# Third step of the common product placed behind P4 of both groups, in the last pair of each SwiGLU

## The chip, the cores and the metric

One core of one Trainium2 chip runs the whole program. The metric is the device time of the program in microseconds, as a median of several runs. Engines are named as the profile names them: PE multiplies matrices, DVE and ACT work on vectors, SP issues the transfers (DMAs).

## The reference

The program is one layer of an encoder block on a sequence of 1024 tokens with 1024 channels, in float32: a SwiGLU, a token-mixing layer (retention and pooling), and a second SwiGLU.

```
h = x + 0.5 * swiglu(rmsnorm(x), ffn1_w_in, ffn1_w_out)
...
h = h + mixing(rmsnorm(h))
h = h + 0.5 * swiglu(rmsnorm(h), ffn2_w_in, ffn2_w_out)
out = rmsnorm(h)

def swiglu(x, w_in, w_out):            # w_in: 1024 x 5632, w_out: 2816 x 1024
    gate, up = split(x @ w_in, 2)
    return (silu(gate) * up) @ w_out
```

The change concerns `x @ w_in`, the first product of each SwiGLU. What it computes is not changed.

## The kernel before

**Three matmuls for one.** Each float32 operand is split into a rounded part and a rest (`split`, lines 160 to 162: a cast on ACT, then a subtraction on DVE). A product of two such operands is three matmuls (`mm3`, lines 181 to 183).

**Groups.** The first product of a SwiGLU makes 22 groups of hidden channels, one by one or in pairs. A group takes two 128-channel tiles (its gate and its up) and all tokens and channels, and is computed by a scheme of Strassen's kind (`strassen`): seven products instead of eight, numbered 1 to 7 and written P1 to P7, each of twelve 512-wide matmuls. Step `A[6]` of a group `A` is P4; it adds into the group's bank `e` and evacuates it, as the (1, 0) quarter, into `au` (line 761). Names in the first SwiGLU begin with `a`, in the second with `c`; the second products (`ffn_out`) are `b` and `d`.

**Pairs and their common product.** Two groups A and B have one more product, P3, in common (`common`): a further split into 2 x 2 smaller blocks saves one of eight. It has three steps, each with a preparation (of weights, on ACT and DVE) and a body (on PE, with the evacuation):

- `one` writes two banks, `x` and `y`, and adds into A's bank `b`.
- `two` finishes A's bank `b`. It also adds `y2` into the lower half of bank `x`, which DVE then reads (line 619, `tt(t["A"][:, HI], x[:, LO], ...)`); then A's `finish` adds bank `b` onto the gate (line 761).
- `three` adds `y4` into B's bank `b` and `y3` into the same half of bank `x`. ACT copies that half (line 627), DVE adds it (line 628), and B's `finish` adds B's bank `b` (line 761).

When both a group's P4 and its `finish` have run, `end` puts its remaining work in a list: the scaling with the norm (line 775), the Silu (line 783), the multiplication with `up` (line 781), and sums and stores for the second product.

**Order.** `pairs_of_both` yields steps in the order in which PE shall do them. `Flow.run` issues the preparation of a step four steps (`LOOK`) before its body, and after each body some of the listed work. A scheduler then sets the order on each engine from these, with the work inside `soon()` (evacuations) ahead of the rest. In all pairs that share P3, `parted` puts A's P4 between `two` and `three`; B's P4 follows.

**Banks.** PE writes into eight banks: six of the pool `ps` and two of the pool `sum` (`N_PS, N_SUM = 6, 2`). A's and B's `b` are the two `sum` banks. The second product begins with four banks `a` (P1) and four banks `b` (P6), which stay in use for all of its eleven steps; the first two `b` banks are the `sum` banks again:

```
bk[where, i] = (sum_bank if where == "b" and i < N_SUM else bank)(f"{name}{n}{where}{i}")
```

A step of the second product is P1 (`bp1a`) and P6 (`bp6b`), twelve matmuls each, three for each bank. Their operands are split by ACT and DVE too (`bp1w`, `bp1m`, `bp6w`, `bp6m` with the number of the step), and lines 906 to 908 make sums of weights.

## Time and profile before

| | |
|---|---|
| median of 3 runs | 2072.68 us (2071.74 to 2073.24) |
| the profiled execution, its own time | 2071.6 us |
| its span in the trace | 2069.8 us |
| granted clock of PE, mean | 0.999 |
| moved by DMAs | 313.57 MB, mean 151 GB/s |

The page of the profile gives busy times by engine, a chain of waits, and groups of instructions. The trace behind it can be asked for the instructions of an engine in order of time (the timeline), for who waited for whom (the waits), and for busy times and the granted clock in stretches (the windows). In a timeline row stand the start and the duration in us, the engine, the line, the operation, its output and inputs (without buffer numbers), and in brackets idle time before it and what ended it. The first SwiGLU's last pair ends at about 407 us of the span, the second's at about 1857 us.

### The profile page before, as it was taken

What the parts mean: (1) busy time and instruction counts of PE and PEld (TensorE: products, weight loads), DVE (VectorE), ACT (ScalarE), POOL (GpSimd) and SP (SyncE); (2) the same over time, 40 slices, a digit from 0 to 9 for tenths busy, and PEclk for the clock granted to TensorE, in tenths of its full rate; (3) what the DMA queues carried; (4) which work ended last, traced back from release to release, by engine and by line L of the source; (5) the groups of instructions that cost most, each with busy time, mean ns of one, the idle gap of its engine ahead of it and who ended that gap; (6) DMA issues with size and microseconds to landing.
All of it is one profiled execution on the core that took longest, in us unless ns stands there. A gap on an engine that the chain in (4) does not pass through costs nothing.

```text
span 2069.8 us, 29688 instructions
## 1 busy us (share of the span) xinstructions
PE 2044.7 (99%) x10672; PEld 1811.1 (87%) x10672; DVE 1835.8 (89%) x3262; ACT 1091.3 (53%) x2061; POOL 0.2 (0%) x4
## 2 busy tenths in 40 slices
PE   9999999999999999999999999999999999999998
PEld 7888989888888888888888999888789999988887
DVE  8799898998996798999778888999989989899897
ACT  8545444554654535454447763456645545455454
POOL 0000000000000000000000000000000000000000
PEclk9999999999999999999999999999999999999999
DMA  7232424576542323243337566724224232457642
GB/s 263 82 138 77 143 87 142 200 265 203 179 151 94 120 106 130 91 143 120 119 128 236 188 234 235 253 92 162 72 86 137 91 136 87 134 207 267 216 145 100
DMA packets 118819, 313.57 MB, mean 151 GB/s; under 512 B 13200, under 2 KB 17424, under 8 KB 118672
## 3 DMA queue, kind: packets, MB, share of 16 engines
q1 hardware_dynamic: 118096, 310.64, 44.4%
q8 instruction: 83, 1.36, 0.3%
q10 hardware_dynamic: 576, 1.05, 0.1%
q14 instruction: 64, 0.52, 0.1%
HBM read 220.93 MB, written 90.70 MB: 151 GB/s over the span
## 4 chain that ended last, share of the span: by engine, by line
PE 74%; DVE 18%; issue 3%; DMA 3%; ACT 3%; SPq 0%; ACTq 0%; DVEq 0%
PE c_b L181 2%; PE c_b L182 2%; PE c_b L183 2%; PE a_b L181 2%; PE a_b L182 2%; PE a_b L183 2%; PE c_e L183 1%; PE c_e L182 1%; PE c_e L181 1%; PE a_e L181 1%; PE a_e L182 1%; PE a_e L183 1%; PE dp5a L181 1%; PE dp5a L182 1%; PE dp5a L183 1%
## 5 line engine op out<-in xcount | busy, mean ns | idle before, releaser
L182 PE MATMUL c_b<-n3T,c_wS 128*128 128x512 f32 x176 | 66.8, 380 | 0.0
L181 PE MATMUL c_b<-n3T,c_wS 128*128 128x512 f32 x176 | 66.5, 380 | 0.2 <-ACT n3T L161 0.2
L183 PE MATMUL c_b<-n3T,c_wS 128*128 128x512 f32 x176 | 66.7, 379 | 0.0
L181 PE MATMUL a_b<-n1T,a_wS 128*128 128x512 f32 x168 | 63.7, 379 | 0.0
L182 PE MATMUL a_b<-n1T,a_wS 128*128 128x512 f32 x168 | 63.7, 379 | 0.0
L183 PE MATMUL a_b<-n1T,a_wS 128*128 128x512 f32 x168 | 63.7, 379 | 0.0
L181 PE MATMUL a_a<-n1R,a_wL 128*128 128x512 f32 x120 | 45.5, 379 | 0.0
L182 PE MATMUL a_a<-n1R,a_wL 128*128 128x512 f32 x120 | 45.5, 379 | 0.0
L183 PE MATMUL a_a<-n1R,a_wL 128*128 128x512 f32 x120 | 45.5, 379 | 0.0
L182 PE MATMUL c_a<-n3R,c_wL 128*128 128x512 f32 x112 | 42.7, 381 | 1.1 <-DVE n3R L166 1.1
L181 PE MATMUL c_a<-n3R,c_wL 128*128 128x512 f32 x112 | 42.6, 380 | 0.8 <-ACT c_b L521 0.8
L183 PE MATMUL c_a<-n3R,c_wL 128*128 128x512 f32 x112 | 42.5, 379 | 0.0
L181 PEld LDWEIGHTS c_b<-n3T,c_wS 128*128 128x128 f32 x176 | 33.2, 189 | 5.1 <-ACT n3T L161 0.6
L182 PEld LDWEIGHTS c_b<-n3T,c_wS 128*128 128x128 f32 x176 | 33.3, 189 | 4.8 <-DVE n3T L162 0.3
L183 PEld LDWEIGHTS c_b<-n3T,c_wS 128*128 128x128 f32 x176 | 33.3, 189 | 4.6
L162 DVE TENSOR_TENSOR a_wS<-a_S,a_wS 128x512 fp32r<-128x512 f32 x45 | 31.3, 697 | 5.0 <-ACT a_wS L161 4.9
L183 PEld LDWEIGHTS a_b<-n1T,a_wS 128*128 128x128 f32 x168 | 31.8, 189 | 4.5
L182 PEld LDWEIGHTS a_b<-n1T,a_wS 128*128 128x128 f32 x168 | 31.8, 189 | 4.3
L181 PEld LDWEIGHTS a_b<-n1T,a_wS 128*128 128x128 f32 x168 | 31.8, 189 | 4.4
L162 DVE TENSOR_TENSOR c_wS<-c_S,c_wS 128x512 fp32r<-128x512 f32 x46 | 32.0, 698 | 2.4 <-ACT c_wS L161 2.3
L161 ACT CAST c_wS<-c_S 128x512 fp32r<-128x512 f32 x46 | 27.8, 622 | 11.4 <-DVE c_S L484 7.0
L182 PE MATMUL c_e<-n3T,c_wL 128*128 128x512 f32 x88 | 33.5, 380 | 0.1
(3159 smaller groups left out, 8034.8 us busy)
## 6 DMA issues: line engine op xcount, KB each, us to landing
c_ra<-in_f_in SPq DMA_DIRECT2D x22, 512.0 KB, 3.7
c_rb<-in_f_in SPq DMA_DIRECT2D x22, 512.0 KB, 3.8
a_ra<-in_f_in SPq DMA_DIRECT2D x21, 512.0 KB, 3.9
a_rb<-in_f_in SPq DMA_DIRECT2D x21, 512.0 KB, 3.8
t<-au SPq DMA_DIRECT2D x11, 512.0 KB, 2.8
b<-ag SPq DMA_DIRECT2D x11, 512.0 KB, 3.7
r<-au SPq DMA_DIRECT2D x11, 512.0 KB, 3.5
bra<-in_f_out SPq DMA_DIRECT2D x11, 512.0 KB, 5.8
```

Of the source, the lines that this page charges most:

```text
L161: copy(hi, src)
L162: tt(lo, src, hi.bitcast(F32), SUB)
L181: mm(dst, w[0], m[0], start=start, stop=False, skip_group_check=True)
L182: mm(dst, w[0], m[1], start=False, stop=False, skip_group_check=True)
L183: mm(dst, w[1], m[0], start=False, stop=stop, skip_group_check=True)
```

## The change

In the last pair of each first product, and only there, the third step of the common product is yielded after the P4 of both groups:

```diff
             yield from (A[1], B[3], B[1], A[2], B[2])
-            if k != some:
+            if n == len(groups) - 2:
+                steps = common(nx, A, B, 3)
+                yield from (*steps[:2], A[6], B[6], steps[2])
+            elif k != some:
                 yield from parted(common(nx, A, B, 3), A[6])
                 yield B[6]
             else:
```

From line 686 on, lines of the changed kernel have numbers higher by 3: line 761 is 764, 775 is 778, 781 is 784, 783 is 786, 908 is 911. Both kernels have the same number of instructions on every engine. Where the orders differ, in each SwiGLU, is from the last P4 to the first steps of the second product. Rows below are those of the first SwiGLU (A is group 10, B is group 21); those of the second read the same with `c` and `d` for `a` and `b`.

On PE, at the end of the first product, before (the last matmul of A's P4, then the first one of each further product; in brackets the engines whose semaphores it waits for):

```order
L183 MATMUL a10_e_3881<-n1T43_754,a10_wL22_3986 128x512
L181 MATMUL a21_b_3822<-n1R22y4_1268,a10_wy3_4003 128x256 [waits DVE_49]
...
L181 MATMUL a10_x3_4023<-n1R22y3_1260,a10_ws343_3967 128x256 [waits DVE_49]
...
L181 MATMUL a21_e_3947<-n1T40_708,a21_wL22_4020 128x512 [waits Activation_49]
...
L181 MATMUL bp1a0_4163<-bp1m0_4055,bp1w0_4052 128x512 [waits Activation_49]
...
L181 MATMUL bp6b1_4194<-bp6m0_4081,bp6w0_4078 128x512 [waits DVE_49,PE_49]
```

and now:

```order
L183 MATMUL a10_e_3881<-n1T43_754,a10_wL22_3986 128x512
L181 MATMUL a21_e_3947<-n1T40_708,a21_wL22_4003 128x512
...
L181 MATMUL a21_b_3822<-n1R22y4_1268,a10_wy3_4020 128x256 [waits Activation_49]
...
L181 MATMUL a10_x3_4023<-n1R22y3_1260,a10_ws343_3967 128x256 [waits DVE_49]
...
L181 MATMUL bp1a0_4163<-bp1m0_4055,bp1w0_4052 128x512 [waits Activation_49]
...
L181 MATMUL bp6b1_4194<-bp6m0_4081,bp6w0_4078 128x512 [waits DVE_49]
```

B's P4 (`a21_e`) moved ahead of the twelve 256-wide matmuls of the third step (`a21_b` with `y4`, `a10_x3` with `y3`), which now stand directly before the second product. The wait of `bp6b1` for DVE is the one for the last reader of B's bank `b`.

On DVE, from the scaling of A's gate to that reader, before:

```order
L775 TENSOR_TENSOR ag10_3832<-ag10_3832,n1rb_961 128x1024 [waits DVE_49]
L628 TENSOR_TENSOR ag21_3833<-a10_x3_4023,ag21_3833 128x256 [waits Activation_49]
L162 TENSOR_TENSOR bp1w1_4103<-bra1_4101,bp1w1_4103 128x512 [waits PE_49]
L761 TENSOR_TENSOR ag21_3833<-a21_b_3822,ag21_3833 128x512 [waits DVE_49]
L781 TENSOR_TENSOR au10_4001<-ag10_3832,au10_4001 128x512 [waits Activation_49]
```

and now:

```order
L778 TENSOR_TENSOR ag10_3832<-ag10_3832,n1rb_961 128x1024 [waits DVE_49]
L911 TENSOR_TENSOR bs32_4183<-bra2_4152 128x512
L764 TENSOR_TENSOR au21_4018<-a21_e_3947,a21_v_3982 128x512 [waits PE_49]
L162 TENSOR_TENSOR bp6m2_4190<-br2_4150,bp6m2_4190 128x512 [waits Activation_49]
L784 TENSOR_TENSOR au10_4001<-ag10_3832,au10_4001 128x512 [waits Activation_49]
L628 TENSOR_TENSOR ag21_3833<-a10_x3_4023,ag21_3833 128x256 [waits Activation_49]
L162 TENSOR_TENSOR bp1w1_4103<-bra1_4101,bp1w1_4103 128x512
L764 TENSOR_TENSOR ag21_3833<-a21_b_3822,ag21_3833 128x512 [waits DVE_49,PE_49]
```

Four instructions that stood behind the evacuation of the third step (a sum of weights, the evacuation of B's P4, a split for the third step's P6, and A's multiplication) now stand ahead of it. Ahead of these rows the only difference is that the rests of `wL22` of B and of `wy3` have changed places.

On ACT, at the same place, before:

```order
L161 CAST bp6w0_4078<-bs20_4073 128x512 [waits DVE_49,PE_49]
L161 CAST bp1w1_4103<-bra1_4101 128x512 [waits DMAHW1_49,DVE_49,PE_49]
L627 COPY ag21_3833<-a10_x3_4023 128x256 [waits PE_49]
L161 CAST bp6w1_4129<-bs20_4073 128x512 [waits DVE_49]
L783 ACTIVATE ag10_3832<-ag10_3832 128x1024 [waits DVE_49,Activation_49]
```

and now:

```order
L161 CAST bp6w0_4078<-bs20_4073 128x512 [waits DVE_49,PE_49]
L161 CAST bp6m2_4190<-br2_4150 128x512
L786 ACTIVATE ag10_3832<-ag10_3832 128x1024 [waits DVE_49,Activation_49]
L161 CAST bp1w1_4103<-bra1_4101 128x512 [waits DMAHW1_49,PE_49]
L627 COPY ag21_3833<-a10_x3_4023 128x256 [waits PE_49]
```

The copy of the third step's result (L627) went from ahead of A's Silu to behind it. On SP the store of `t` (from `au21`) and the load of the seventh step's `br` have changed places.

## Prediction

> **What bounds the kernel now.** I read the totals first, then the waits of the matmul engine, then the order of time around the places that the change touches.

> ```profile
> span 2069.8 us, 29688 instructions
> PE 2044.7 (99%) x10672; PEld 1811.1 (87%) x10672; DVE 1835.8 (89%) x3262; ACT 1091.3 (53%) x2061; POOL 0.2 (0%) x4
> PE 74%; DVE 18%; issue 3%; DMA 3%; ACT 3%; SPq 0%; ACTq 0%; DVEq 0%
> ```

> PE is busy 99% of the span. A change that keeps the same matmuls can therefore only move PE's waits. DVE is close behind with 89%, so these waits are mostly waits for DVE. In the view of PE's waits (who waited for whom; total, times, longest) two rows belong to the step that is moved, and a third to a later stage:

> ```profile
> PE vL L182 <- DVE vL11w L162: 1.5, 1, 1.5
> PE a_x L181 <- DVE ag L619: 1.3, 1, 1.3
> PE c_x L181 <- DVE cg L619: 1.0, 1, 1.0
> ```

> There is one such wait per SwiGLU, and each has its place in the last pair: PE must not add `y3` into bank `x` before DVE has read the old content (L619). The timeline of PE at the first place (start, duration, instruction, and in brackets the idle time before it):

> ```profile
> 401.91 0.27 PE L181 MATMUL a_b<-n1R22y,a_wy 128*128 128x256 f32 x1
> 402.02 0.28 PE L182 MATMUL a_b<-n1R22y,a_wy 128*128 128x256 f32 x1
> ...
> 402.46 0.28 PE L183 MATMUL a_b<-n1R22y,a_wy 128*128 128x256 f32 x1
> 404.03 0.38 PE L181 MATMUL a_x<-n1R22y,a_ws 128*128 128x256 f32 x1 [1.29 <-DVE ag L619]
> ...
> 404.80 0.38 PE L181 MATMUL a_e<-n1T,a_wL 128*128 128x512 f32 x1
> ...
> 407.40 0.38 PE L181 MATMUL bp1a<-bp1m,bp1w 128*128 128x512 f32 x1
> ...
> 410.63 0.38 PE L181 MATMUL bp6b<-bp6m,bp6w 128*128 128x512 f32 x1
> ```

> Matmuls overlap, so I count starts and not durations. A 256-wide one takes 0.11 us from start to start (401.91 to 402.02), and twelve 512-wide ones take 2.60 us (404.80 to 407.40), or 0.216 each. The row at 410.63 is the second bank of the next product, `bp6b1`; the matmuls ahead of it are the twelve of `bp1a` and three of `bp6b0`.

> **The change, part by part.** No instruction is added or removed in either SwiGLU. In each, P4 of the second group (twelve matmuls, 2.60 us) moves ahead of the third step (twelve 256-wide matmuls), and DVE, ACT and SP are reordered to suit.

> *The wait that goes.* From the last `a_b` start at 402.46 to the first `a_e` at 404.80 is 2.34 us. Seven undisturbed starts take 7 x 0.111 = 0.78 us, so the wait really costs 1.56 us: the 1.29 that is named, the drain of the pipeline and a slow first matmul. With B's P4 ahead, PE reaches `y3` at 401.91 + 2.60 + 0.67 = 405.18. DVE's read ends at 403.56 + 0.42 = 403.98 (row below), and the rows ahead of it on DVE are the same set as before, two of them swapped. The wait goes completely, and B's P4 is the work that hides it. The second place:

> ```profile
> 1852.58 0.28 PE L183 MATMUL c_b<-n3R22y,c_wy 128*128 128x256 f32 x1
> 1853.85 0.38 PE L181 MATMUL c_x<-n3R22y,c_ws 128*128 128x256 f32 x1 [1.00 <-DVE cg L619]
> ...
> 1854.62 0.38 PE L181 MATMUL c_e<-n3T,c_wL 128*128 128x512 f32 x1
> ...
> 1860.45 0.38 PE L181 MATMUL dp6b<-dp6m,dp6w 128*128 128x512 f32 x1
> ```

> There it is 1854.62 - 1852.58 - 0.78 = 1.26 us. Taken alone, the two waits are a gain of 2.82 us.

> *The wait that comes.* The third step is now the last work of the first product, and its evacuation is what the second product waits for. Bank `b` of group B is one of the two sum banks. `bp6b1` takes it over, so its first matmul waits until DVE has read it (in the third step's evacuation, the add into `ag21`, line 761 before and 764 after). DVE before, at the first place:

> ```profile
> 403.56 0.42 DVE L619 TENSOR_TENSOR ag<-a_x,ag 128x256 f32<-128x256 f32 x1
> ...
> 406.89 1.22 DVE L775 TENSOR_TENSOR ag<-ag,n1rb 128x1024 f32<-128x1024 f32 x1
> 408.02 0.42 DVE L628 TENSOR_TENSOR ag<-a_x,ag 128x256 f32<-128x256 f32 x1
> 408.35 0.69 DVE L162 TENSOR_TENSOR bp1w<-bra,bp1w 128x512 fp32r<-128x512 f32 x1
> 408.95 0.69 DVE L761 TENSOR_TENSOR ag<-a_b,ag 128x512 f32<-128x512 f32 x1
> 409.55 0.69 DVE L781 TENSOR_TENSOR au<-ag,au 128x512 f32<-128x512 f32 x1
> ```

> Here the read ends at 408.95 + 0.69 = 409.64, and PE needs the bank at 410.63: 0.99 us to spare, so the trace shows no wait. After the change both sides move against each other. PE comes earlier by the 1.56 us: `y3` ends at about 405.85, `bp1a` takes 2.60 and three matmuls of `bp6b0` 0.65, so it reaches `bp6b1` at 409.09. DVE comes later: the order of the changed kernel puts four 512-wide instructions between the scaling (line 778) and L628, namely line 911, the add of B's P4, a `bp6m2` split and line 784. One takes 0.60 us from start to start (408.95 to 409.55), so four take 2.40. The read then ends at 409.64 + 2.40 = 412.04, and PE starts about 0.05 later (403.98 to 404.03 above), at 412.09. The new wait is 412.09 - 409.09 = **3.00 us**, against 1.56 saved: net **+1.46 us**, or simply `bp6b1` at 412.09 instead of 410.63.

> At the second place DVE has the same order, and the same start to start:

> ```profile
> 1853.38 0.42 DVE L619 TENSOR_TENSOR cg<-c_x,cg 128x256 f32<-128x256 f32 x1
> ...
> 1858.78 0.69 DVE L761 TENSOR_TENSOR cg<-c_b,cg 128x512 f32<-128x512 f32 x1
> ```

> The read ends at 1858.78 + 0.69 + 2.40 = 1861.87, `dp6b1` starts at 1861.92 instead of 1860.45: +1.47. The sum doesn't depend on when DVE starts: if it comes some tenths earlier or later, the old wait and the new one move together, as long as both exist.

> *What could stretch it.* ACT must keep up with DVE. In the new order the copy L627, which L628 waits for, stands behind the Silu and a cast:

> ```profile
> 408.20 1.06 ACT L783 ACTIVATE ag<-ag 128x1024 f32<-128x1024 f32 x1 [2.31 <-DVE ag L775]
> 409.17 0.60 ACT L161 CAST bp1w<-bra 128x512 fp32r<-128x512 f32 x1
> ```

> The Silu still waits for the scaling, so it starts at 408.20, the cast at 409.17, the copy at about 409.7, done at 410.1. DVE gets to line 784 (needs the Silu, done at 409.26) at 409.82 and to L628 at 410.42. Both are covered by 0.3 to 0.5 us; if the cover were gone by as much again, each place would cost up to 0.4 us more. The other end is that nothing stretches: I take that, and keep +0.8 for the range. SP only exchanges a store of `au` with a load of `br`; both queue positions are next to each other, and the loaded rows are for the seventh step of the second product. Each step is 24 matmuls of 0.216 us, 5.2 us, so I cost the exchange at nothing: six steps of PE work hide it.

> *What is late next.* DVE's split for `bp6` of the third step and the rest of the group's work shift by about 1.2 us, but PE is later by more, and after these instructions both orders are the same again. Nothing there becomes a wait. No PE wait follows in the first SwiGLU's second product. DVE even idles for PE-paced work before its end:

> ```profile
> 517.12 0.69 DVE L162 TENSOR_TENSOR bp5w<-bs,bp5w 128x512 fp32r<-128x512 f32 x1 [1.90 <-ACT bp5w L161]
> ```

> so lateness of PE is handed on to the mixing stage in full.

> *Sum.* Gains -1.56 - 1.26, new waits +3.00 + 2.73, net +2.9 us. The span goes from 2069.8 to 2072.7, the profiled execution's own time from 2071.6 to 2074.5. The median of the runs is 2072.68, 1.1 above that execution; moved by the same 2.9 it becomes **2075.6**. That is +0.14%. I count 0.2%, 4.1 us, as what a measurement of this kernel can tell from no change, so the likeliest answer is a small loss within that bound.

> **Rivals.** *Only the old waits go* (chance 0.09). The bank comes free in time because DVE runs the pieces faster than before or PE waits for another bank. For it speaks the 0.99 us of slack in the trace of before; against it, that slack is used up by PE's gain alone (1.56), before DVE's 2.40. It would give 2072.68 - 2.8 = 2069.9, which is also where a change that does just what it says ends.

> *The lateness is absorbed* (0.15). The row on `vL` above is a wait of 1.5 us for DVE at the next stage. If DVE's chain there doesn't depend on PE, a PE that comes 1.46 later loses nothing at the first place; the second place still counts. That gives 2072.68 + 1.5 = 2074.1, and 2072.7 if the same happens there. Against it speaks DVE's idle row at 517.12.

> *The clock falls in the new wait* (0.07), the case clearly slower than before. The trace has one place where PE stops for long, the end (stretch, PE busy and count, then the others; the granted clock stands behind POOL):

> ```profile
> 2062.11 0.38 PE L183 MATMUL dp5a<-dp4w,dp4m 128*128 128x512 f32 x1
> 2064.00:2065.00 1.00, 0.00 (x0) 0.00 (x0) 0.77 (x4) 0.73 (x2) 0.00 (x0) 1.00 0.91 346
> 2065.00:2066.00 1.00, 0.00 (x0) 0.00 (x0) 0.93 (x3) 0.59 (x1) 0.00 (x0) 0.84 0.70 274
> 2066.00:2067.00 1.00, 0.00 (x0) 0.00 (x0) 0.16 (x1) 0.13 (x1) 0.00 (x0) 0.50 0.65 250
> ```

> The last matmul ends at 2062.49, and 0.84 means that the clock was halved about two thirds into its microsecond, at 2065.7: after 3.2 us of idleness. My new waits, less the tail of the last matmul (0.38 - 0.22), are 2.84 and 2.57 us: under it, but by only 0.4 at the first. If the clock fell and stayed low as long as the idleness that caused it, 3.2 us, it would cost 1.6 us a place: 2075.6 + 3.2 = 2078.8. It decides from a wait of some 3.2 us on.

> [...]

> **How the numbers follow.** The forecast has 0.66. Something I don't see has 0.03. The forecast's own range is 2.9 us, up to 0.8 more, on runs that scatter from 2071.74 to 2073.24: 2074.4 to 2077.1. To hold 8 in 10 I add the absorbed cases, down to 2072.7 and below that by the scatter, to 2071.5, and leave a little above, to 2077.8. Left out are the pure gain, the clock and the unseen: 0.19. Slower by over 0.2% (above 2076.8) is the clock's 0.07, 0.05 from the upper edge of the forecast and 0.02 unseen: 0.14. Faster by over 0.2% (below 2068.5) is the lower edge of the gain and the unseen: 0.03. The rest, 0.83, is within 0.2%.

> **What would show it.** In the changed kernel's waits, the rows for `a_x` and `c_x` on L619 must be gone. In their place there must be rows of `bp6b` and `dp6b` waiting for DVE's `ag` and `cg` on line 764, near 3.0 and 2.7 us. `bp6b1` should start 1.46 us later than 410.63. DVE's read of `a_b` should end near 412.04, with the four named instructions ahead of L628. The granted clock behind the new waits should stay at 1.00, and starts at 0.216. I am wrong if PE passes `bp6b1` without a wait, if the wait at `vL` shrinks by what was lost before it, or if matmuls behind the wait start 0.43 us apart.

## The result and the profile after

| | before | changed |
|---|---|---|
| median of 7 runs of each, taken together | 2071.92 us (2070.93 to 2073.31) | 2078.04 us (2076.43 to 2081.23) |
| ratio, 95% interval | | 1.0029 (1.0020 to 1.0039) |
| the profiled execution, its own time | 2071.6 us | 2077.55 us |
| its span in the trace | 2069.8 us | 2075.8 us |

The change makes the kernel slower by 6.0 us (4.1 to 8.1). Differences in us, here and below, are worked out from the ratio, which need not be that of the two medians. Two executions with a granted clock of 0.53 and 0.56 (8790.51 us of one experiment, 3599.26 us of the kernel before) are left out of the ratios below. The forecast was 2.9 us and 2075.6; the median lies 0.24 us above the upper end of the range, 2077.8.

The head of the changed kernel's page, first:

```profile
span 2075.8 us, 29686 instructions
...
PE 2047.0 (99%) x10672; PEld 1811.0 (87%) x10672; DVE 1836.2 (88%) x3262; ACT 1091.7 (53%) x2061; POOL 0.2 (0%) x4
```

The number of matmuls is the same, but PE is busy for 2.3 us longer (2044.7 before). Waiting alone can't do that: some matmuls must have taken longer. PE's waits (who waited for whom; total, times, longest):

```profile
PE dp6b L181 <- DVE cg L764: 3.1, 1, 3.1
PE bp6b L181 <- DVE ag L764: 2.7, 1, 2.7
PE vL L182 <- DVE vL11w L162: 2.0, 1, 2.0
```

The rows of `a_x` and `c_x` on L619 are gone, and the two new waits are where the prediction put them. Now the first place, PE and then DVE, in order of time:

```profile
405.48 0.38 PE L181 MATMUL bp1a<-bp1m,bp1w 128*128 128x512 f32 x1
...
408.50 0.38 PE L183 MATMUL bp6b<-bp6m,bp6w 128*128 128x512 f32 x1
411.57 0.48 PE L181 MATMUL bp6b<-bp6m,bp6w 128*128 128x512 f32 x1 [2.69 <-DVE ag L764]
411.89 0.38 PE L182 MATMUL bp6b<-bp6m,bp6w 128*128 128x512 f32 x1
412.10 0.38 PE L183 MATMUL bp6b<-bp6m,bp6w 128*128 128x512 f32 x1
```

```profile
406.35 1.22 DVE L778 TENSOR_TENSOR ag<-ag,n1rb 128x1024 f32<-128x1024 f32 x1
407.49 0.69 DVE L911 TENSOR_TENSOR bs<-bra 128x512 f32<-128x512 f32 x1
408.09 0.69 DVE L764 TENSOR_TENSOR au<-a_e,a_v 128x512 f32<-128x512 f32 x1
408.69 0.69 DVE L162 TENSOR_TENSOR bp6m<-br,bp6m 128x512 fp32r<-128x512 f32 x1
409.29 0.69 DVE L784 TENSOR_TENSOR au<-ag,au 128x512 f32<-128x512 f32 x1
409.89 0.42 DVE L628 TENSOR_TENSOR ag<-a_x,ag 128x256 f32<-128x256 f32 x1
410.23 0.69 DVE L162 TENSOR_TENSOR bp1w<-bra,bp1w 128x512 fp32r<-128x512 f32 x1
410.82 0.69 DVE L764 TENSOR_TENSOR ag<-a_b,ag 128x512 f32<-128x512 f32 x1
```

DVE works without a break, with the four named rows, 2.40 us, between L778 and L628. Its read ends at 411.51, and PE starts 0.06 later. Everything here stands about 0.5 us earlier than I wrote, since DVE began earlier in this execution; the differences are as forecast. The second place (PE, then stretches in the order of the windows: length, PE busy and number of matmuls, PEld, DVE, ACT, POOL, granted clock, DMA share, GB/s):

```profile
1861.19 0.38 PE L183 MATMUL dp6b<-dp6m,dp6w 128*128 128x512 f32 x1
1864.72 0.79 PE L181 MATMUL dp6b<-dp6m,dp6w 128*128 128x512 f32 x1 [3.15 <-DVE cg L764]
1865.30 0.63 PE L182 MATMUL dp6b<-dp6m,dp6w 128*128 128x512 f32 x1
1865.73 0.63 PE L183 MATMUL dp6b<-dp6m,dp6w 128*128 128x512 f32 x1
...
1868.37 0.38 PE L181 MATMUL dp1a<-dp1m,dp1w 128*128 128x512 f32 x1
```

```profile
407.09:410.51 3.42, 1.79 (x9) 1.23 (x7) 3.42 (x7) 2.84 (x6) 0.00 (x0) 1.00 0.40 134
410.51:413.92 3.41, 2.35 (x11) 2.09 (x12) 3.41 (x6) 2.11 (x5) 0.00 (x0) 1.00 0.40 142
...
1861.17:1864.59 3.42, 0.40 (x2) 0.00 (x0) 3.42 (x8) 3.42 (x7) 0.00 (x0) 1.00 0.34 73
1864.59:1868.00 3.41, 3.28 (x8) 2.65 (x9) 3.41 (x6) 2.08 (x4) 0.00 (x0) 0.50 0.22 89
```

Behind the second wait the matmuls start 0.43 us apart instead of 0.216, and the granted clock is 0.50 for 3.41 us. Behind the first it stays at 1.00. That is the sign that I had named for being wrong. Why at one place and not at the other, with waits of 3.15 and 2.69 us, is what the experiments are about.

### The profile page after: what moved, and what is told of

Read it like the earlier page. It is cut to its first block, busy times and chain, and to the rows that moved or that the text cites. A ratio compares the mean times of both kernels' runs of the same rounds, so it can differ in the third digit from the quotient of the medians.

```text
span 2075.8 us, 29686 instructions
## 1 busy us (share of the span) xinstructions
PE 2047.0 (99%) x10672; PEld 1811.0 (87%) x10672; DVE 1836.2 (88%) x3262; ACT 1091.7 (53%) x2061; POOL 0.2 (0%) x4
## 4 chain that ended last, share of the span: by engine, by line
PE 76%; DVE 16%; ACT 3%; issue 3%; DMA 2%; SPq 0%; ACTq 0%; DVEq 0%
PE c_b L181 2%; PE c_b L182 2%; PE c_b L183 2%; PE a_b L181 2%; PE a_b L182 2%; PE a_b L183 2%; PE c_e L183 2%; PE c_e L182 2%; PE c_e L181 2%; PE a_e L181 1%; PE a_e L183 1%; PE a_e L182 1%; PE c_a L182 1%; PE c_a L181 1%; PE c_a L183 1%
## 5 line engine op out<-in xcount | busy, mean ns | idle before, releaser
L182 PE MATMUL c_b<-n3T,c_wS 128*128 128x512 f32 x176 | 66.8, 380 | 0.0
L181 PE MATMUL c_b<-n3T,c_wS 128*128 128x512 f32 x176 | 66.5, 380 | 0.2 <-ACT n3T L161 0.2
L183 PE MATMUL c_b<-n3T,c_wS 128*128 128x512 f32 x176 | 66.7, 379 | 0.0
L181 PE MATMUL a_b<-n1T,a_wS 128*128 128x512 f32 x168 | 63.7, 379 | 0.0
L182 PE MATMUL a_b<-n1T,a_wS 128*128 128x512 f32 x168 | 63.7, 379 | 0.0
L183 PE MATMUL a_b<-n1T,a_wS 128*128 128x512 f32 x168 | 63.7, 379 | 0.0
L181 PE MATMUL a_a<-n1R,a_wL 128*128 128x512 f32 x120 | 45.5, 379 | 0.0
L183 PE MATMUL a_a<-n1R,a_wL 128*128 128x512 f32 x120 | 45.5, 379 | 0.0
L182 PE MATMUL a_a<-n1R,a_wL 128*128 128x512 f32 x120 | 45.5, 379 | 0.0
L182 PE MATMUL c_a<-n3R,c_wL 128*128 128x512 f32 x112 | 42.7, 381 | 1.1 <-DVE n3R L166 1.1
L181 PE MATMUL c_a<-n3R,c_wL 128*128 128x512 f32 x112 | 42.6, 380 | 0.8 <-ACT c_b L521 0.8
L183 PE MATMUL c_a<-n3R,c_wL 128*128 128x512 f32 x112 | 42.4, 379 | 0.0
L181 PEld LDWEIGHTS c_b<-n3T,c_wS 128*128 128x128 f32 x176 | 33.2, 189 | 5.1 <-ACT n3T L161 0.6
L182 PEld LDWEIGHTS c_b<-n3T,c_wS 128*128 128x128 f32 x176 | 33.3, 189 | 4.8 <-DVE n3T L162 0.3
L183 PEld LDWEIGHTS c_b<-n3T,c_wS 128*128 128x128 f32 x176 | 33.3, 189 | 4.7
L183 PEld LDWEIGHTS a_b<-n1T,a_wS 128*128 128x128 f32 x168 | 31.8, 189 | 4.5
L181 PEld LDWEIGHTS a_b<-n1T,a_wS 128*128 128x128 f32 x168 | 31.8, 189 | 4.4
L182 PEld LDWEIGHTS a_b<-n1T,a_wS 128*128 128x128 f32 x168 | 31.8, 189 | 4.4
L162 DVE TENSOR_TENSOR a_wS<-a_S,a_wS 128x512 fp32r<-128x512 f32 x45 | 30.8, 686 | 5.0 <-ACT a_wS L161 5.0
L161 ACT CAST c_wS<-c_S 128x512 fp32r<-128x512 f32 x46 | 27.8, 623 | 11.3 <-DVE c_S L484 6.9
L162 DVE TENSOR_TENSOR c_wS<-c_S,c_wS 128x512 fp32r<-128x512 f32 x46 | 31.6, 688 | 2.4 <-ACT c_wS L161 2.3
L182 PE MATMUL c_e<-n3T,c_wL 128*128 128x512 f32 x88 | 33.5, 380 | 0.1
```

The source lines that it names most:

```text
L161: copy(hi, src)
L162: tt(lo, src, hi.bitcast(F32), SUB)
L181: mm(dst, w[0], m[0], start=start, stop=False, skip_group_check=True)
L182: mm(dst, w[0], m[1], start=False, stop=False, skip_group_check=True)
L183: mm(dst, w[1], m[0], start=False, stop=stop, skip_group_check=True)
```

## The experiments

To compare places, I count from the first matmul of A's P4 to the 84th matmul behind it, well past the wait (before: 399.32 to 417.75 and 1849.43 to 1867.58), and take the difference from before. "Half" says whether the clock was halved behind the wait; the last column is DVE's idle time for the DMA of `bra` or `dra` ahead of the place (before: 1.39 and 1.10).

```
execution              place   longer by   PE's wait there     half   DVE's idle for the DMA
changed                first    +1.40      2.69                no     1.21
changed, once more     first    +2.89      2.69                yes    1.23
first only             first    +3.07      2.67                yes    1.19
P4 in halves           first    +2.58      2.16                yes    1.22
with matmuls inside    first    +1.42      none shown          no     1.23
banks turned           first    +0.99      0.84+0.62+0.28      no     2.09
changed                second   +3.76      3.15                yes    1.67
changed, once more     second   +3.42      2.72                yes    1.25
second only            second   +1.63      2.62                no     1.14
P4 in halves           second   +1.19      2.16                no     1.18
with matmuls inside    second   +2.18      0.44                no     1.78
banks turned           second   +0.57      0.62+0.28           no     1.38
first only (old order) second   +0.16      1.16, on L619       no     1.25
```

**One place alone.** The edits, each in a kernel of its own:

```diff
-            if n == len(groups) - 2:
+            if n == len(groups) - 2 and nx.name == "n1":
```

```diff
-            if n == len(groups) - 2:
+            if n == len(groups) - 2 and nx.name == "n3":
```

> The new order in the first SwiGLU only; the second one as before. Theory 1 (each place costs the net of its waits, some 1.4 us, and the halved clock comes on top in some executions, when the wait of PE grows past about 3 us): a wait of bp6b for DVE's ag on L764 of 2.7 to 3.0 us, and no wait of dp6b on L764; before +1.4 us, up to +3 in an execution in which the clock halves there. Rival (the loss belongs to the second place and whatever stands around it, the first is free): no change from before, within 0.5 us.

> The new order in the second SwiGLU only. Theory 1: a wait of dp6b for DVE's cg on L764 of 2.7 to 3.2 us; before +1.4 us in executions with the full clock, +3 to +3.8 in those where the granted clock is 0.50 for some 3.4 us behind the wait. This and the first place alone should add up to the whole change. Rival (the second place carries the whole loss): before +5 to +6 us.

The first place alone: 2074.30 us beside 2072.25 of before, ratio 1.0010 (1.0001 to 1.0018), +2.1 us. The second alone: 2074.45, ratio 1.0014 (1.0005 to 1.0022), +2.9 us. By time alone the rival with a free first place isn't excluded, since the interval of the first begins at 0.2 us. The profile excludes it: with only the first place changed, that place is longer by 3.07 us. The second place alone doesn't cost the rival's 5 to 6 us either (1.0 to 4.6). So both places cost. The first place of the kernel with only that changed (PE, and the windows):

```profile
411.35 0.48 PE L181 MATMUL bp6b<-bp6m,bp6w 128*128 128x512 f32 x1 [2.67 <-DVE ag L764]
```

```profile
408.41:411.83 3.42, 0.75 (x4) 0.46 (x3) 3.42 (x8) 3.42 (x9) 0.00 (x0) 1.00 0.48 152
411.83:415.24 3.41, 3.41 (x9) 2.71 (x9) 3.41 (x6) 1.70 (x4) 0.00 (x0) 0.50 0.02 7
```

This breaks theory 1 in one point. A wait of 2.67 us halved the clock here; one of 2.69 us didn't in the changed kernel. And in the kernel with only the second place changed, 2.62 us didn't:

```profile
1863.14 0.48 PE L181 MATMUL dp6b<-dp6m,dp6w 128*128 128x512 f32 x1 [2.62 <-DVE cg L764]
```

```profile
1859.00:1862.41 3.41, 1.52 (x8) 0.98 (x6) 3.41 (x8) 3.17 (x6) 0.00 (x0) 1.00 0.35 107
1862.41:1865.82 3.41, 2.68 (x12) 2.38 (x13) 3.41 (x6) 2.09 (x5) 0.00 (x0) 1.00 0.35 125
```

So it isn't the length of the wait alone. The trace keeps the start and the length of each stretch of the granted clock. The one at half clock in the changed kernel lasts 3.413 us, the full clock ahead of it 1860.264 us and behind it 204.800 us, which are 545 and 60 times 3.41333. Counted from the start of the first stretch at full clock, in units of 3.41333 us:

```
execution             full clock from   half clock from (us, units)         for
before                4.04              2065.68 (604.0)                     to the end
changed               4.32              1864.58 (545.0)                     3.413
changed, once more    5.04              411.22 (119.0), 1865.30 (545.0)     3.413, 3.413
first only            5.64              411.82 (119.0)                      3.413
second only           5.56              1398.20 (408.0)                     3.413
with matmuls inside   6.27              1398.91 (408.0)                     3.413
banks turned          5.32              1397.96 (408.0)                     3.413
P4 in halves          5.94              412.12 (119.0), 1398.57 (408.0)     3.413, 3.413
```

Every one begins at a whole number of units, and those inside a kernel last one. (Each of the others has one more at its end, as `before` has.) The start of the count differs between executions by about 2 us (4.04 to 6.27). That made theory 2, which is what the windows above are cut by: the clock is set anew every 3.413 us, by how busy PE was in the unit before. Of all units of these eight executions at full clock, those followed by half clock had at most 1.59 us of PE work, and those followed by full clock at least 1.50. A wait is called caught when the unit behind it runs at half clock. The wait of the changed kernel's first place is cut in two by the boundary at 410.51 and leaves PE 1.79 us of work in one unit and 2.35 in the next; that of the kernel above lies in one unit whole and leaves 0.75.

**Matmuls inside the wait.** In each place, eleven more matmuls:

```diff
+N_FILL = 11
...
                     mm3(bk[where, i], parts(o["w"], i), moving(o["m"]), start and k == 0, k == FH - 1)
+                    if n == "p6" and k == 0 and i == 0:
+                        for z in range(N_FILL):
+                            mm(bk[where, 3], parts(o["w"], 1)[0], moving(o["m"])[0], start=True, stop=True, skip_group_check=True)
```

> The changed kernel with eleven matmuls more at each place, between bp6b0 and bp6b1 (dp6b0 and dp6b1), into bank 3, which the next product starts afresh, so their result is overwritten. They take 11 x 0.216 = 2.4 us, less than the wait. PE isn't idle there any more, but bp6b1 still starts when DVE has read the bank. Theory 1 (the wait costs 1.4 us a place, the clock the rest): no halved clock at either place, idle times under 1 us, before +2.9 us, runs scattered no wider than those of before. Rival A (the clock has nothing to do with idleness, or the loss is DVE's lateness alone): as the changed kernel, +5 to +6 us. Rival B (PE had no room for it): more than the changed kernel by up to 2 x 2.4 us.

Measured: 2076.39 us, ratio 1.0021 (1.0013 to 1.0030), +4.4 us. The eleven matmuls at the second place, and the windows of both places:

```profile
1862.63 2.64 PE L977 MATMUL dp6b<-dp6m,dp6w 128*128 128x512 f32 x11 [0.44 <-DVE cu L765]
```

```profile
408.94:412.35 3.41, 3.32 (x14) 2.47 (x14) 3.41 (x8) 3.41 (x9) 0.00 (x0) 1.00 0.49 148
...
1862.57:1865.98 3.41, 3.26 (x14) 2.56 (x15) 3.41 (x8) 3.41 (x8) 0.00 (x0) 1.00 0.43 149
```

PE works through the wait, the clock stays at 1.00 at both places, and yet the first is longer by 1.42 us, the same as the changed kernel's 1.40 without halving. So the wait and the clock are two terms, and the wait's is the 1.46 of the prediction. Rival B falls: the matmuls cost nothing of their own. Rival A falls by the profile, where the clock holds at both places; by time alone it would not, for the interval of this kernel (2.7 to 6.2 us) reaches its 5 to 6, and a gain over the changed kernel isn't clear of the scatter. The sum of 4.4 is over my 2.9, at the edge of its interval. In the profiled execution 0.7 us of that is the second place, where DVE waited 0.68 us longer for the DMA than before, and 0.5 us a halved clock at 1398.91, in the mixing stage, which is no part of the change. Whether the other runs have the same extra isn't shown.

**Banks asked for in another order.**

```diff
-                for i in range(4):
+                for i in (0, 3, 2, 1) if n == "p6" and k == 0 else range(4):
```

> The changed kernel, but the first step of the second product's sixth part (bp6, dp6) takes the banks in the order 0, 3, 2, 1 instead of 0, 1, 2, 3, so that the bank that DVE frees last is asked for last. Theory 1: the wait is cut into up to three shorter ones, of at most 1.1 us each; the step ends at about 412.75 in the time of the first place, against 412.58 before and 414.03 in the changed kernel, so before +0.2 us a place, +0.4 in all, no row on L764 over 1.2 us and no halved clock. Rival (what costs is that DVE is done later, and whatever hangs on DVE's end, not the order in which PE asks for banks): as the changed kernel, +3 to +6 us.

Measured: 2073.50 us, ratio 1.0007 (0.9998 to 1.0016), +1.5 us, with zero in the interval. At the first place:

```profile
410.23 0.48 PE L181 MATMUL bp6b<-bp6m,bp6w 128*128 128x512 f32 x1 [0.84 <-DVE au L764]
...
411.77 0.48 PE L181 MATMUL bp6b<-bp6m,bp6w 128*128 128x512 f32 x1 [0.62 <-DVE ag L628]
...
412.97 0.48 PE L181 MATMUL bp6b<-bp6m,bp6w 128*128 128x512 f32 x1 [0.28 <-DVE ag L764]
```

```profile
408.09:411.51 3.42, 2.22 (x10) 1.28 (x8) 3.42 (x6) 2.44 (x5) 0.00 (x0) 1.00 0.13 53
```

The one wait has become three short ones, no unit is left with less than 2.22 us of work, and the clock holds. The places are longer by 0.99 and 0.57 us, against 0.2 worked out; at the first, DVE idled 0.70 us longer for its DMA than before, at the second 0.28, and that is most of the difference. The same four DVE rows are ahead of the bank's read, so what the order of the banks saves is only the matmuls that PE does in the meantime. It brings the changed kernel back to about the kernel before, not ahead of it: DVE has no gap here that PE could use.

**The changed kernel once more, and pauses by themselves.**

> The changed kernel once more, for its sum and one more look at its two places. Theory 2 (the clock is set anew in a fixed grid of windows of 3.413 us, counted from the start of the full clock; a window in which the matmuls fill less than about half is followed by one at half clock; whether a wait of 2.7 to 3.1 us is caught depends on where it lies in the grid): every half stretch that the records show begins at a whole multiple of 3.413 us and lasts 3.413 us, at either place or at neither; before +2.9 us of waits and 0 to 1.7 us for each place caught, +4 to +6 in the median. Rival (a wait halves the clock when it is longer than about 3 us, wherever it lies): only a wait over 3 us is followed by half clock, none under it.

> A kernel that leaves out the whole computation: 180 bursts of 32 to 47 matmuls of 512, each followed by a pause of PE while DVE copies 128 to 2560 columns of the bank, twenty lengths of pause from some 0.4 to 3.5 us, nine times each, at places in the grid that come out by chance. Theory 2: no pause under about 1.7 us is followed by half clock; from about 1.8 us on half of them are, and 80% at 3.0 us, those that take 1.8 us or more out of one window of the grid; the half clock lasts exactly one window of 3.413 us. Rival (a fixed length of idleness decides): none below 3.0 to 3.4 us, all above.

The changed kernel: 2077.67 us, beside 2072.12 of before; ratio 1.0026 (1.0017 to 1.0035), +5.4 us. This time both places were caught, the first with the wait of 2.69 us that wasn't caught before:

```profile
411.58 0.79 PE L181 MATMUL bp6b<-bp6m,bp6w 128*128 128x512 f32 x1 [2.69 <-DVE ag L764]
412.17 0.63 PE L182 MATMUL bp6b<-bp6m,bp6w 128*128 128x512 f32 x1
```

```profile
407.81:411.22 3.41, 1.09 (x6) 0.60 (x4) 3.41 (x7) 3.41 (x7) 0.00 (x0) 1.00 0.34 93
411.22:414.63 3.41, 3.05 (x7) 2.50 (x8) 3.41 (x6) 2.09 (x4) 0.00 (x0) 0.50 0.26 106
```

Between the two executions the boundary moved from 410.51 to 411.22, and the wait, at the same time of the span, now leaves one unit with 1.09 us of work. The rival (only a wait over 3 us) falls with it: both waits here, 2.69 and 2.72 us, are shorter and are caught. The first place is longer by 2.89 instead of 1.40: 1.49 us is the price of being caught.

The kernel of pauses is a loop of its own; its core (`n` counts the bursts, `g` the twenty lengths of pause, the copies on DVE are the pause of PE):

```
for z in range(BURST + (5 * n) % 16):
    mm(b, w[:, (z % 4) * P : (z % 4 + 1) * P], m, start=z == 0, stop=True, skip_group_check=True)
width = (g + 1) * GAP_STEP
while width:
    c = min(width, H)
    d = sb.tile([P, H], F32, tag="d", bufs=4, name="d")
    nc.vector.tensor_copy(d[:, :c], b[:, :c])
    width -= c
```

Its 52 stretches at half clock all begin at whole numbers of units, within 2 ns. Of the 51 before the end, 44 last one unit and 7 two; "exactly one window" was expected, so the 7 are a miss. They are those in which the first unit at half clock had at most 2.81 us of PE work; in the 44 it had at least 2.89. By the length of the pause (start to start, less 0.38 us for the last matmul, which is the idle time that a row names):

```
pause            pauses   followed by half clock
0.4 to 1.7 us      90        0
1.8 to 2.2 us      27       10
2.3 to 2.6 us      27       15
2.8 to 3.2 us      35       26
```

Two pauses of the same 2.44 us, and the units around them:

```profile
398.45 1.80 PE L122 MATMUL b<-m,w 128*128 128x512 f32 x4 [2.44 <-DVE d L127]
...
1785.35 0.97 PE L122 MATMUL b<-m,w 128*128 128x512 f32 x3 [2.44 <-DVE d L127]
```

```profile
395.37:398.79 3.42, 0.98 (x5) 0.49 (x4) 2.35 (x4) 0.00 (x0) 0.00 (x0) 1.00 0.00 0
398.79:402.20 3.41, 3.41 (x10) 2.65 (x9) 0.00 (x0) 0.00 (x0) 0.00 (x0) 0.50 0.00 0
1781.18:1784.60 3.42, 1.72 (x8) 1.10 (x6) 1.66 (x3) 0.00 (x0) 0.00 (x0) 1.00 0.00 0
1784.60:1788.01 3.41, 2.66 (x12) 2.19 (x13) 0.69 (x2) 0.00 (x0) 0.00 (x0) 1.00 0.00 0
```

The first pause lies in one unit, the second across a boundary. Over all pauses, a unit at full clock with less than 1.2 us of PE work was always followed by half clock, one with more than 1.6 never. In between there are some of both kinds. The theory's outline holds, and the first pauses caught, of 1.85 us, are where it had them. Two of its numbers were a little off: it had the limit at about half a unit, 1.71 us, where no unit with more than 1.6 us was followed by half clock, and 80% at 3.0 us, where it is 26 of 35. The rival of a fixed length has no place for 25 pauses caught below 2.7 us.

**B's P4 in two halves.**

```diff
-        def b4():
-            prod("e", "L22", "T4", False, True)
-            with soon():
-                evac((1, 0), t["e"], t["v"])
+        def b4(some=range(4)):
+            for i in some:
+                mm3(t["e"], parts(t["w", "L22"], i), moving(nx.operand("T4", i)), False, i == 3)
+            if 3 in some:
+                with soon():
+                    evac((1, 0), t["e"], t["v"])
...
+        g.parts = [lambda: b4((0, 1)), last(lambda: b4((2, 3)))]
...
-                yield from (*steps[:2], A[6], B[6], steps[2])
+                yield from (*steps[:2], A[6], (B[6][0], B.parts[0]), steps[2], (lambda: None, B.parts[1]))
```

> The changed kernel with B's P4 in two halves of six matmuls, one ahead of the common's third step and one behind it, an attempt to keep PE's gain. PE alone would give before -0.95 us a place: a wait for L619 of 0.2 us instead of 1.3. But on DVE the reading add of the bank b then stands behind three 512-wide rows more than in the kernel before, 1.8 us: theory 1 (the order on DVE decides) has bp6b1 and dp6b1 wait for the add of ag and cg by some 2.2 us, before +0.9 us a place, +1.7 in all, and up to 1.7 us more for each place where the clock halves. Rival (DVE's order is of no account, its rows run when PE needs them): before -1.9 us.

Measured: 2075.64 us, ratio 1.0015 (1.0005 to 1.0024), +3.1 us. The waits are what DVE's order gave, at both places:

```profile
411.26 0.45 PE L181 MATMUL bp6b<-bp6m,bp6w 128*128 128x512 f32 x1 [2.16 <-DVE ag L767]
...
1864.39 0.45 PE L181 MATMUL dp6b<-dp6m,dp6w 128*128 128x512 f32 x1 [2.16 <-DVE cg L767]
```

```profile
408.71:412.12 3.41, 1.25 (x6) 0.82 (x5) 3.41 (x7) 3.41 (x8) 0.00 (x0) 1.00 0.04 18
412.12:415.54 3.42, 3.42 (x10) 2.71 (x9) 3.42 (x6) 2.22 (x4) 0.00 (x0) 0.50 0.00 0
1862.79:1866.20 3.41, 1.80 (x9) 1.62 (x10) 3.41 (x6) 3.02 (x6) 0.00 (x0) 1.00 0.00 0
```

Two waits of the same 2.16 us, one caught and one not: longer by 2.58 and by 1.19 us. The second is near the 0.9 worked out from rows alone, and the rival (-1.9 us) falls. The attempt to keep PE's gain failed for the same reason as the change: more rows on DVE ahead of the awaited one, three here. None of the versions beats the kernel before.

## Why the prediction was wrong

**The wait that goes: right.** The rows on L619 are gone in both profiled executions of the changed kernel.

**The wait that comes: right, mechanism and size.** Foretold were waits of 3.00 and 2.73 us by start times, at `bp6b1` and `dp6b1`, for DVE's `ag` and `cg` on L764, behind four named rows of 2.40 us, and +1.46 us a place. Measured without halving: +1.40, +1.42, +1.63 and +2.18 us. DVE's idle time for the DMA was shorter by 0.18 and 0.16 us than before in the first two, and longer by 0.04 and 0.68 in the others. Without that they are 1.58, 1.58, 1.59 and 1.50, some 0.1 over the forecast. The sum left out that the first matmul behind the wait is slow: 0.32 us to the next start (411.57 to 411.89) instead of 0.216. The waits that the trace names are shorter than mine, as the last matmul's 0.38 is not counted as waiting: 411.57 - 408.50 - 0.216 = 2.85 us by starts.

**"The sum doesn't depend on when DVE starts": right, with a remark.** DVE's late DMAs are paid in full, but they are paid in the kernel before too, where PE waits for L619: with the old order, a DMA that came 0.15 us later made the second place longer by 0.16.

**What is late next: right.** The wait at `vL` is 2.0 us and 1.4 us in the two executions of the changed kernel, 1.5 before; it didn't shrink by what was lost ahead of it, so the rival in which the lateness is absorbed falls.

**The clock: wrong, and this is the step that failed.** I read from one row that the clock falls "after 3.2 us of idleness", set the point from which it decides at "a wait of some 3.2 us", put my waits "under it", and gave the case 0.07. The one row, at the end of the kernel before, couldn't show that: its half clock starts at 2065.68, a whole number of units from the start of the count, and the 3.2 us from the last matmul are merely where that matmul happened to lie. What told the waits at the two places apart was the work that they left in one unit of 3.413 us: 0.40 to 1.25 us in the five that were caught, 1.52 to 1.80 in the three that weren't. By the pauses, a wait like mine is caught in about 6 of 10 cases (15 of 27 at 2.3 to 2.6 us, 26 of 35 from 2.8 us); of the eight waits of 2.16 to 3.15 us in the table above, five were. The price, foretold as 1.6 us, came out at 1.49 to 1.67 us at the first place (2.89 and 3.07 less 1.40). The reason given for it was wrong, and the size is luck: at both places the half clock lasted one unit, 3.413 us, behind waits of 2.16 to 3.15 us alike, and not as long as the wait. The old waits of 1.0 and 1.3 us named are among the lengths of which none of 90 was caught, so this term is new with the change.

**The sum.** With the waits 2.9 us and two places caught 6 times in 10 at about 1.55 us, it would have been 2.9 + 1.9 = 4.8 us. Measured are 6.0 (4.1 to 8.1) and 5.4 (3.5 to 7.3). In the first profiled execution 1.40 + 3.76 of the 6.0 us are in the two places; the rest, 0.8 us, lies elsewhere, with 0.5 of it in the wait at `vL`, and executions of the kernel before differ by more among themselves (2070.93 to 2073.31). That the range was also drawn too narrow is the same mistake: the case clearly slower was priced at 2078.8, and would have had to be inside.

## What to carry to other kernels

Where an engine works without a break and another waits for it, moving the other's work only moves the wait: look at which rows will stand ahead of the awaited one on the busy engine, and count those. And two waits of 1.3 us are not the same as one of 2.7: in this kernel the waits that left PE 0.40 to 1.25 us of work in one unit of 3.413 us were followed by half clock, a second loss of 1.49 to 1.67 us where a wait of 2.7 us was measured with and without it; those that left 1.52 us or more were not. A long wait can therefore be worth cutting in pieces, even when it doesn't become shorter in sum: with the banks in another order, or with eleven matmuls inside, the clock held at both places, behind units with at least 2.22 and 3.26 us of PE work.
